# A first load in two parts by partitions, and a reworked tail, in a loss kernel bound by its loads

## Chip, cores, metric

One core of a Trainium2 chip. The metric is the device time of one execution in microseconds; profiles are of single executions, whose span (first to last instruction) is some 2 us shorter.

## The reference

```python
# pred, target: (32, 147, 768) float32
mean = target.mean(axis=-1, keepdims=True)
var = target.var(axis=-1, keepdims=True)
target = (target - mean) / np.sqrt(var + 1e-6)
loss = np.mean((pred - target) ** 2, axis=-1)
return loss.mean(axis=-1)          # 32 numbers
```

Each row of 768 numbers is normalised, subtracted, squared and averaged. Both inputs are read once, 28.90 MB, and 32 numbers are written.

## The kernel before

The 128 partitions are 32 batches x 4 rows; partition 4b + j holds rows 37j and onward of batch b, one row of 768 per "column" c. Columns 0 to 35 fill all partitions, a last one (REST) fills 96. The first four target columns and REST come in float32 from SyncE's queue (the hardware queue); all else goes through GpSimd's queue (the software queue), which converts to bf16 (13.52 MB written there for 27.03 read).

```python
def load(kind, c0, c1, d0, d1, q):
    ...
    til = data.tile([P, (c1 - c0) * w], F32 if q == "hw" else BF16, ...)
    src = bass.AP(tensor=x.tensor, offset=x.offset + c0 * D + d0,
                  ap=[[N * D, B], [KJ * D, J - 1 if c0 == REST else J], [1, (c1 - c0) * w]])
    pin((nc.sync if q == "hw" else nc.gpsimd).dma_start(out=til[:n], in_=src))
...
# statistics on VectorE (two bn_stats and a bn_aggr a column), root on ScalarE,
# normalisation on GpSimd; then, for most columns, TensorE adds -target and +pred
# through identity matrices into PSUM, and ScalarE squares and sums:
    nc.scalar.activation(out=z[:n, :w], in_=z[:n, :w], func=ACTF.Square, accum_out=dest[:n])
# columns 31 and 34 are VectorE's: difference in bf16, then
def mean_of_squares(u, dest):
    z = zs[u]
    mv = small.tile([P, 2], F32, name="mvz")
    bn(mv, [z[:, 0:half], z[:, half:D]])
    nc.vector.scalar_tensor_tensor(out=dest, in0=mv[:, 0:1], scalar=mv[:, 0:1], in1=mv[:, 1:2],
                                   op0=ALU.mult, op1=ALU.add)
...
# at the end a few products with masks sum over partitions, a copy, a store of 128 bytes
```

A small list scheduler in the program orders each engine's instructions by estimated times. The last column (35) is loaded and squared in pieces of 512 and 256.

## Time and profile before

| | before |
|---|---|
| median time | 77.87 us (77.81 to 78.01) |
| span of the profile | 75.9 us |
| first DMA packet | 2.24 us |
| last load's last increment | 72.19 us |
| VectorE, GpSimd, TensorE, ScalarE busy | 66%, 69%, 50%, 42% |
| read from memory | 28.90 MB |

How to read it: no compute engine is near full, the DMA row is. So only what happens before the DMA engines run, how fast they run, and what follows the last landing can move the time. The semaphore of a load of 32 batches rises sixteen times in the trace (the hardware queue's two loads and the store give 16 + 16 + 1 = 33 semaphore writes); this text takes an increment as the share of one of the core's 16 DMA engines, and how far the sixteen lie apart as a sign of how even the engines are. No trace names the engine of a packet or of an increment, so "twelve engines" below means twelve increments. The lines themselves stand in the prediction.

### The profile page before, as it was taken

The numbers are of one execution on the slowest core, as the hardware profiler recorded it, in microseconds if no ns is written. First come the engines' busy times: TensorE is split into PE (matmuls) and PEld (weight loads), VectorE is DVE, ScalarE is ACT, GpSimd is POOL, SyncE is SP. The second block draws the span as 40 slices with busy tenths as digits, with TensorE's granted clock in tenths as the row PEclk, the third lists the DMA queues.
The fourth block names the chain that finished last, engine by engine and source line by source line (L and its number), as shares of the span: only waits on it lengthen the run. The fifth ranks groups of instructions, "written<-read, shape, count | busy, mean of one in ns | idle before, by whom it ended". The sixth has DMA issues, their size and how long they took to land.

```text
span 75.9 us, 638 instructions
## 1 busy us (share of the span) xinstructions
PE 38.2 (50%) x128; PEld 11.5 (15%) x128; DVE 50.2 (66%) x137; ACT 32.0 (42%) x67; POOL 52.6 (69%) x78
## 2 busy tenths in 40 slices
PE   0000000046884865507682877197517978774860
PEld 0000000011222221102110212031102213212230
DVE  0000399999999999997079609941999891019770
ACT  5100000400259519502940096019522963995850
POOL 4998205299999489899399508960999998992000
PEclk9999999999999999999555558955985558999999
DMA  0899999999999999999999999999999999999500
GB/s 0 207 414 330 243 230 236 220 210 207 214 214 223 214 221 210 207 214 217 217 220 217 211 207 217 227 210 196 212 214 214 209 212 213 203 211 200 86 0 0
DMA packets 4118, 15.43 MB, mean 203 GB/s; under 512 B 466, under 2 KB 1458, under 8 KB 3986
## 3 DMA queue, kind: packets, MB, share of 16 engines
q0 software_dynamic: 3856, 13.52, 88.8%
q1 hardware_dynamic: 258, 1.87, 6.9%
q14 instruction: 3, 0.02, 0.1%
q8 instruction: 1, 0.02, 0.1%
HBM read 28.90 MB, written 0.00 MB: 381 GB/s over the span
## 4 chain that ended last, share of the span: by engine, by line
DMA 62%; DVE 13%; POOL 13%; issue 3%; PE 2%; ACT 2%; POOLq 0%; DVEq 0%; ACTq 0%
DMA p<-in_pred_dram 52%; DMA t<-in_target_dram 11%; POOL s L212 10%; DVE st L162 10%; POOL p L108 2%; PE z L226 2%; ACT z L238 2%; DVE mv L163 2%; DVE zd L245 1%; POOL t L108 1%; PE acc L294 0%; DVE r L192 0%; DVE rl L251 0%; DVE mvz L163 0%; ACT r L186 0%
## 5 line engine op out<-in xcount | busy, mean ns | idle before, releaser
L212 POOL TENSOR_SCALAR s<-t,nm,r 128x768 bf16<-128x768 bf16 (+2 forms) x37 | 36.0, 979 | 9.7 <-DVE r L192 7.5
L162 DVE BATCH_NORM_STATS2 st<-t 128x6 f32<-128x384 bf16 (+2 forms) x74 | 36.2, 530 | 9.3 <-DMA t<-in_target_dram 9.3
L238 ACT ACTIVATE z<-z 128x1536 f32<-128x1536 f32 (+4 forms) x21 | 25.7, 1223 | 22.9 <-PE z L226 22.9
L226 PE MATMUL z<-s,nident 128*128 128x512 bf16 (+3 forms) x55 | 19.5, 460 | 25.5 <-POOL s L212 17.8
L226 PE MATMUL z<-p,ident 128*128 128x512 bf16 (+3 forms) x55 | 19.0, 476 | 9.8 <-DMA p<-in_pred_dram 9.7
L108 POOL DMA_DIRECT2D p<-in_pred_dram x18 | 10.3, 575 | 1.0 <-DVE r L192 0.3
L186 ACT ACTIVATE r<-mv,eps_t 128x4 f32<-128x4 f32 (+2 forms) x12 | 3.5, 289 | 17.7 <-DVE mv L163 17.0
L226 PEld LDWEIGHTS <-nident 128*128 128x128 bf16 (+1 forms) x55 | 4.6, 107 | 39.5 <-ACT z L238 18.1
L226 PEld LDWEIGHTS <-ident 128*128 128x128 bf16 (+1 forms) x55 | 6.4, 117 | 20.3 <-issue 17.7
L108 POOL DMA_DIRECT2D t<-in_target_dram x9 | 5.4, 605 | 4.8 <-DMA t<-in_target_dram 3.8
L163 DVE BATCH_NORM_AGGREGATE mv<-st 128x2 f32<-128x12 f32 (+1 forms) x37 | 7.7, 209 | 1.3
L192 DVE RECIPROCAL r<-r 128x4 f32<-128x4 f32 (+2 forms) x12 | 1.7, 143 | 9.3 <-ACT r L186 9.2
L238 ACT ACTIVATION_READ_ACCUMULATOR z<-z 128x1 f32 (+1 forms) x21 | 4.0, 189 | 0.0
L245 DVE TENSOR_TENSOR zd<-p,s 128x768 bf16<-128x768 bf16 x2 | 1.9, 944 | 2.5 <-POOL s L212 2.1
L151 DVE TENSOR_SCALAR mask_mean<-mask 128x32 f32<-128x32 f32 x1 | 2.7, 2731 | 0.0
L187 ACT ACTIVATE nm<-mv 128x4 f32<-128x4 f32 (+2 forms) x12 | 2.3, 191 | 0.0
L162 DVE BATCH_NORM_STATS2 st<-zd 128x6 f32<-128x384 bf16 x4 | 2.0, 552 | 0.1
L186 ACT ACT_TABLE_LOAD x1 | 1.3, 1283 | 0.8 <-PEq L340 0.8
L294 PE MATMUL acc<-mask,rl 128*1 128x32 f32 x10 | 1.1, 192 | 0.2 <-ACT z L238 0.2
L148 DVE MEMSET eps_t<- 128x1 f32 x1 | 0.1, 59 | 0.9 <-PEq L340 0.9
L294 PEld LDWEIGHTS acc<-mask,rl 128*1 128x1 f32 x10 | 0.5, 82 | 0.5 <-ACT z L238 0.3
L294 PE MATMUL acc<-mask_mean,rl 128*1 128x32 f32 x4 | 0.4, 190 | 0.1
(23 smaller groups left out, 4.7 us busy)
## 6 DMA issues: line engine op xcount, KB each, us to landing
t<-in_target_dram POOLq DMA_DIRECT2D x7, 768.0 KB, 26.3
p<-in_pred_dram POOLq DMA_DIRECT2D x5, 768.0 KB, 29.1
p<-in_pred_dram POOLq DMA_DIRECT2D x5, 384.0 KB, 20.0
t<-in_target_dram SPq DMA_DIRECT2D x1, 1536.0 KB, 8.0
p<-in_pred_dram POOLq DMA_DIRECT2D x5, 192.0 KB, 12.3
t<-in_target_dram POOLq DMA_DIRECT2D x2, 384.0 KB, 24.6
t<-in_target_dram SPq DMA_DIRECT2D x1, 288.0 KB, 10.4
p<-in_pred_dram POOLq DMA_DIRECT2D x1, 144.0 KB, 10.6
```

Of the source, the lines that this page charges most:

```text
L108: pin((nc.sync if q == "hw" else nc.gpsimd).dma_start(out=til[:n], in_=src))
L151: op("mask_mean", "DVE", 0.2, ["masks"], lambda: pin(nc.vector.tensor_scalar(out=mask_mean, in0=mask, scalar1=float(D), scalar2=None, op0= ...
L162: pin(nc.vector.bn_stats(out=st[:n, j, :], in_=x))
L163: pin(nc.vector.bn_aggr(out=out, in_=st[:n, :len(parts)]))
L186: pin(nc.scalar.activation(out=r[:n], in_=mv[:n, :, 1], func=ACTF.Sqrt, bias=eps_t[:n], scale=1.0))
L187: pin(nc.scalar.activation(out=nm[:n], in_=mv[:n, :, 0], func=ACTF.Copy, scale=-1.0))
L192: pin(nc.vector.reciprocal(out=rs[g][:n], in_=rs[g][:n]))
L212: pin(nc.gpsimd.tensor_scalar(out=s[:n, so:so + D], in0=til[:n, o:o + D], scalar1=nm, scalar2=r, op0=ALU.add, op1=ALU.mult))
L226: pin(nc.tensor.matmul(z[:n, a:b], eye[:n, :n], src[:n, so + a:so + b], start=first, stop=not first))
L238: pin(nc.scalar.activation(out=z[:n, :w], in_=z[:n, :w], func=ACTF.Square, accum_out=dest[:n]))
L245: pin(nc.vector.tensor_tensor(out=z, in0=til[:, o:o + D], in1=s[:, so:so + D], op=ALU.subtract))
L294: pin(nc.tensor.matmul(acc, vec[:n], m[:n], start=len(turn) == 1, stop=len(turn) == len(finals)))
```

## The change

Its intent: the first load in two parts (its first packets sooner), a shorter chain on VectorE for its tail columns, the last column in equal halves with a PSUM tile of its own, and roots placed ahead of squares that still wait. The core of it:

```diff
+        if not tbuf:
+            h = B // 4
+            for a, b in ((0, h), (h, B)):
+                part = bass.AP(tensor=x.tensor, offset=src.offset + a * N * D,
+                               ap=[[N * D, b - a], [KJ * D, J], [1, (c1 - c0) * w]])
+                pin(eng.dma_start(out=til[a * J:b * J], in_=part))
+        else:
+            pin(eng.dma_start(out=til[:n], in_=src))
...
-    piece("p", KM - 1, KM, 0, BANK)
-    piece("p", KM - 1, KM, BANK, D)
+    piece("p", KM - 1, KM, 0, half)
+    piece("p", KM - 1, KM, half, D)
...
-        mv = small.tile([P, 2], F32, name="mvz")
-        bn(mv, [z[:, 0:half], z[:, half:D]])
-        (multiply and add of mean and variance into dest)
+        pin(nc.vector.scalar_tensor_tensor(out=z, in0=z, scalar=1.0, in1=z, op0=ALU.mult, op1=ALU.mult,
+                                           accum_out=dest))
...
-            key = (t, rank, i)
+            key = (t - (1.0 if name[0] == "root" else 0.0), rank, i)
```

Cut: the scheduler's landing estimates (some 0.7 us later), the last piece's own PSUM tile, and the removal of a mask scaled by 768.

More of the change, by code (lines that the diff above doesn't have):

```diff
@@ L87 @@
     units += [((KM - 6 + i,), 0, D, eng) for i, eng in enumerate(("ACT", "DVE", "ACT", "ACT", "DVE"))]
-    units += [((KM - 1,), 0, BANK, "ACT"), ((KM - 1,), BANK, D, "ACT")]
+    units += [((KM - 1,), 0, half, "ACT"), ((KM - 1,), half, D, "ACT")]
     ops, by_name = [], {}
@@ L107, in load @@
                       ap=[[N * D, B], [KJ * D, J - 1 if c0 == REST else J], [1, (c1 - c0) * w]])
-        pin((nc.sync if q == "hw" else nc.gpsimd).dma_start(out=til[:n], in_=src))
+        eng = nc.sync if q == "hw" else nc.gpsimd
+        if not tbuf:
[6 more added lines that the diff above has]
+            pin(eng.dma_start(out=til[:n], in_=src))
         for c in range(c0, c1):
             KIND[kind].setdefault(c, []).append((d0, d1, til, (c - c0) * w))
-    land, lanes, clock, last = {}, {"hw": [], "sw": []}, 2.5, {}
+    land, lanes, clock, last = {}, {"hw": [], "sw": []}, 2.9, {}
     for i, (kind, c0, c1, d0, d1, q) in enumerate(stream):
         w = (c1 - c0) * (d1 - d0)
-        clock += w * rows_of(c0) / P * 0.915 / D + 0.03
-        lanes[q].append(clock + 0.8)
+        clock += w * rows_of(c0) / P * 0.915 / D + (0.0 if w >= 4 * D else 0.04)
+        lanes[q].append(clock + 1.1)
         for c in range(c0, c1):
-            land[kind, c, d0] = clock + 0.8
+            land[kind, c, d0] = clock + 1.1
         k = len(lanes[q])
@@ L130 @@
     mask_rest = singles.tile([P, B], F32)
-    mask_mean = singles.tile([P, B], F32)
     eps_t = singles.tile([P, 1], F32)
@@ L150 @@
     op("masks", "POOL", 3.0, [], masks, early=3.0)
-    op("mask_mean", "DVE", 0.2, ["masks"], lambda: pin(nc.vector.tensor_scalar(
-        out=mask_mean, in0=mask, scalar1=float(D), scalar2=None, op0=ALU.mult)), rank=99.0)
     mvs = {}
@@ L228, in sub_target @@
     def sub_target(u, d0, w):
-        zs[u, d0] = psum.tile([P, 3 * BANK], F32, name="z")
+        if (u, d0) == units[-1][:2]:
+            zs[u, d0] = psum1.tile([P, BANK], F32, name="z_last")
+        else:
+            zs[u, d0] = psum.tile([P, 3 * BANK], F32, name="z")
         s, so = sbuf[u[0]]
@@ L245, in difference, with square_dve @@
         pin(nc.vector.tensor_tensor(out=z, in0=til[:, o:o + D], in1=s[:, so:so + D], op=ALU.subtract))
-    def mean_of_squares(u, dest):
+    def square_dve(u, dest):
         z = zs[u]
-        mv = small.tile([P, 2], F32, name="mvz")
-        bn(mv, [z[:, 0:half], z[:, half:D]])
-        pin(nc.vector.scalar_tensor_tensor(out=dest, in0=mv[:, 0:1], scalar=mv[:, 0:1], in1=mv[:, 1:2],
-                                           op0=ALU.mult, op1=ALU.add))
+        pin(nc.vector.scalar_tensor_tensor(out=z, in0=z, scalar=1.0, in1=z, op0=ALU.mult, op1=ALU.mult,
+                                           accum_out=dest))
     n_early = sum(1 for u, d0, d1, eng in units if len(u) == 2)
@@ L271 @@
             dest = singles.tile([P, 1], F32, name=f"rl{k}")
-            finals.append((("sq", k), dest, mask_rest if u[0] == REST else mask if eng == "ACT" else mask_mean,
+            finals.append((("sq", k), dest, mask_rest if u[0] == REST else mask,
                            rows_of(u[0])))
@@ L275 @@
             op(("diff", k), "DVE", 0.6, norms, lambda u=u: difference(u), rank=-2.0, early=arrive)
-            op(("sq", k), "DVE", 1.5, [("diff", k)], lambda u=u, dest=dest: mean_of_squares(u, dest), rank=-70.0)
+            op(("sq", k), "DVE", 1.0, [("diff", k)], lambda u=u, dest=dest: square_dve(u, dest), rank=-70.0)
             continue
-        op(("subt", k), "PE", 0.37 * w / D, norms + users[-2:-1] + ["ident"],
+        op(("subt", k), "PE", 0.37 * w / D, norms + (users[-2:-1] if k < len(units) - 1 else []) + ["ident"],
            lambda u=u, d0=d0, w=w: sub_target(u, d0, w), rank=k + 0.0)
@@ L296 @@
     for i, (need, vec, m, n) in enumerate(finals):
-        op(("final", i), "PE", 0.2, [need, "masks", "mask_mean"], lambda v=vec, m=m, n=n: final(v, m, n), rank=90.0)
+        op(("final", i), "PE", 0.2, [need, "masks"], lambda v=vec, m=m, n=n: final(v, m, n), rank=90.0)
     HOP = 0.15
@@ L310 @@
             t = max([free[engine], early] + [end[x] + (0.0 if ops[by_name[x]][1] == engine else HOP) for x in needs])
-            key = (t, rank, i)
+            key = (t - (1.0 if name[0] == "root" else 0.0), rank, i)
             if best is None or key < best[0]:
-                best = (key, i)
-        (t, _, _), i = best
+                best = (key, i, t)
+        _, i, t = best
         name, engine, dur, needs, fn, rank, early = ops[i]
```

## The prediction

> **What bounds the kernel now.** I read the page first, then the chain that ended last in order of time, then the timeline of both ends, then the single DMA packets in the trace. The page:
>
> ```profile
> DVE  0000399999999999997079609941999891019770
> POOL 4998205299999489899399508960999998992000
> DMA  0899999999999999999999999999999999999500
> ...
> q0 software_dynamic: 3856, 13.52, 88.8%
> q1 hardware_dynamic: 258, 1.87, 6.9%
> ...
> HBM read 28.90 MB, written 0.00 MB: 381 GB/s over the span
> ...
> DMA 62%; DVE 13%; POOL 13%; issue 3%; PE 2%; ACT 2%; POOLq 0%; DVEq 0%; ACTq 0%
> ```
>
> The DMA row stands at 9 from the third of its forty slices to the thirty-seventh, while VectorE (66% of the span) and GpSimd (69%) have holes. So the kernel is the time before the DMA engines run, the time they need for 28.90 MB, and what comes after the last landing. The packets give the rate: a 12,288-byte packet takes 0.460 to 0.475 us on its engine, from 3.4 us on and in both queues (a software packet writes 6,144 bytes because it converts to bf16, but reads 12,288). Eight such packets per engine are one load of four columns, and those loads land 3.66 us apart (16.23, 19.87, 23.53 us and so on): 0.458 us a packet. Each engine thus runs back to back at 12,288/0.46 = 26.7 GB/s, sixteen of them at 427 GB/s. No engine has room to take over another's work.
>
> The end, in the timeline:
>
> ```profile
> 71.29 0.56 DVE L245 TENSOR_TENSOR zd<-p,s 128x768 bf16<-128x768 bf16 x1 [0.37 <-DMA p<-in_pred_dram]
> ...
> 71.88 1.02 DVE L162 BATCH_NORM_STATS2 st<-zd 128x6 f32<-128x384 bf16 x2
> 71.90 0.38 PE L226 MATMUL z<-p,ident 128*128 128x512 bf16 x1
> ...
> 72.37 0.58 ACT L238 ACTIVATE z<-z 128x512 f32<-128x512 f32 x1 [0.22 <-PE z L226]
> ...
> 72.54 0.27 PE L226 MATMUL z<-p,ident 128*128 128x256 bf16 x1
> ...
> 72.96 0.38 ACT L238 ACTIVATE z<-z 128x256 f32<-128x256 f32 x1
> ...
> 73.18 0.22 DVE L251 SCALAR_TENSOR_TENSOR rl<-mvz 128x1 f32<-128x1 f32 x1
> 73.26 0.19 ACT L238 ACTIVATION_READ_ACCUMULATOR z<-z 128x1 f32 x1
> 73.45 0.09 PEld L294 LDWEIGHTS acc<-mask_mean,rl 128*1 128x1 f32 x2 [0.26 <-DVE rl L251]
> ...
> 73.51 0.22 PE L294 MATMUL acc<-mask,rl 128*1 128x32 f32 x2
> 73.77 0.18 DVE L322 COPY ob<-acc 1x32 f32<-1x32 f32 x1 [0.37 <-PE acc L294]
> ```
>
> (I left out lines between.) Column 34 lands at 71.19 us and goes through VectorE until 73.40; the two pieces of column 35 land at 71.86 and 72.19 and go through TensorE and ScalarE until 73.45. **Two chains end within 0.05 us of each other**, so shortening one alone gives nothing. From the last landing to the end of the span it is 75.9 - 72.19 = 3.7 us, of which 2.4 are the last product, the output's copy and its store.
>
> The sixteen increments of the last load's semaphore arrive between 71.08 and 71.73 us, but for one at 72.19: an engine that carried a 16,384-byte instruction fetch at 67.77 us for 0.95 us. It is late from then on.
>
> The start, in the timeline:
>
> ```profile
> 0.81 1.31 SPq L108 DMA_DIRECT2D t<-in_target_dram  x2
> ...
> 8.86 1.02 DVE L162 BATCH_NORM_STATS2 st<-t 128x6 f32<-128x384 f32 x2 [7.92 <-DMA t<-in_target_dram]
> ```
>
> The first packet moves at 2.24 us; packets of the software queue join at 5.74 us, and from there the two queues alternate. The first load has landed at 8.84.
>
> [...] the 258 hardware packets are 128 + 96 of data, one store and 33 semaphore writes, 16 + 16 + 1. [...] the subtraction of column 31, begun at 67.96 beside GpSimd, took 1.33 us, that of column 34 with GpSimd idle 0.56.
>
> **The change part by part.**
>
> First load in two. The parts' patterns begin with 8 and 24 batches. [...] Before, every engine had 128/16 = 8. [...] All later loads are spread evenly and every engine is full to the end, [...] 4 x 0.46 = **1.84 us on every later landing**, the last one included. What may be won back: the first packets of before took about 1 us instead of 0.46 with all sixteen starting at once, and a shorter first issue or fewer starters may save up to 0.4; I put 0.2. And if the engine with the instruction fetch isn't among the eight, the last landing is 71.73 + 1.84 at most instead of 72.19 + 1.84, that is 0.46 less; at even odds 0.23. Shift of the last landing: 1.84 - 0.2 - 0.23 = +1.4 us.
>
> The first load itself: 101 of its 128 packets had begun by 5.74, 6.3 per engine. After, 5.7 of 12 would be left, alternating with software packets at 0.94 a pair: 5.4 us, so it lands at about 11.3 instead of 8.84. VectorE starts 2.5 us late. It has some 26 us idle in the span, and loses the mask multiplication (2.7 us in the table of groups, once), so this is hidden.
>
> VectorE's tail columns. Removed per column: two statistics (1.02), an aggregation (0.22), a small multiply (0.23), with gaps 1.53 us. Added: one multiply over 768 elements with accumulation. Estimate: the statistics run 384 elements in 0.53 and the one-element multiply takes 0.22, [...] plus 0.1 to 0.2 for reading the accumulator: 1.15. Saves about 0.4 us on the chain of column 34, which then ends near 73.0 on before's clock, off the path.
>
> Last column in halves. ScalarE took 0.58 for 512 and 0.38 for 256 columns; 384 is 0.48. With L the last landing, the first half lands near L - 0.5 and its square runs from L - 0.03 to L + 0.45; the second half's product (0.33 and some 0.1 of delay) is ready at L + 0.47, its own PSUM tile sparing it a wait; square and accumulator read end at L + 1.2, against 73.45 - 72.19 = 1.26 before. Gain 0.05 to 0.2; I take 0.15.
>
> Roots ahead of waiting squares, and later estimated landings: these change orders only. Products and squares in the middle have slack against the DMA engines, so 0.
>
> Sum: 77.87 + 1.4 - 0.15 = **79.1 us**.
>
> **Rivals.**
> First, the load is spread over all sixteen engines after all. For it: the new estimates of landing in the program (2.9 and 1.1 us) agree with before's measured landings within some 0.1 us, as if the split had moved nothing. [...] Then the tail alone counts: 77.5 to 77.8.
> Second, the engines share a bound, so that the others go faster [...]. [...] Against it: the constant 0.46 us a packet. It would make about 78.
> Third, GpSimd stalls on issues: it waits in order for the eighth-last load to land, and the program now expects landings 1.8 us too early. Its last normalisation ended at 68.88, 2.3 us before column 34 landed, so I see little; if it bites, 79.5 to 80.
> Fourth, the tail's gain is larger (roots unblock ScalarE, 0.3 us more). It can't reach the 1.56 us that a gain of 2% needs.
>
> **Range and chances.** I give the uneven spread 80%. Within it the time runs from 78.7 (start and fetch both kind) to 79.7, and 2% slower is 79.43, so about a third of it is beyond. The rest lies at 77.4 to 78.2. Range 77.5 to 79.7; slower 0.27, same 0.69, faster 0.04.
>
> **What would show it.** Semaphore writes of the hardware queue: 8 + 12 + 16 + 1 = 37 if the spread is uneven, 49 if all parts use sixteen engines. Increments of the later loads then spread over some 4 us or more instead of 0.5, and loads land about 1.6 us later from 16 us to the end. The first statistics begin near 11 us. In the tail there is one multiply of about 1 us and an accumulator read in place of four instructions, VectorE is done before ScalarE, and the last square ends 1.2 us after the last landing. The prediction is wrong if the landings in the middle stand where they stood, or if the tail after the last landing changes by over 0.4 us.

Its sum came to 77.87 + 1.4 - 0.15 = 79.1 us. The four extra packets behind the 1.84 in that 1.4 have lost their derivation: the prediction took 12 packets of the first load for eight engines, 8 for four and none for four from an assumption that no trace had shown by then. The result shows the counts: the two parts' semaphores rise 8 and 12 times, and later loads have twelve late increments and four on time. The middle step of the multiply's estimate (1.0 us) assumed a fixed time per instruction that is not measured; that multiply is not in the sum.

## The result

84.1 us median (83.7 to 84.88, 6 runs) against 77.86 before: ratio 1.0813, 95% interval 1.0765 to 1.0861. A ratio here is the mean time of one kernel's fast runs over that of the other's fast runs of the same rounds, so not quite the ratio of the medians. The change is 6.2 us slower; 1.2 were predicted.

The page of the changed kernel (VectorE's and the DMA engines' busy tenths, the queues, the chain that ended last):

```profile
DVE  0000000009999999995995970893399974015520
DMA  0699999999999999999999999999999999998300
...
q1 hardware_dynamic: 262, 1.87, 10.4%
...
HBM read 28.90 MB, written 0.00 MB: 347 GB/s over the span
...
DMA 65%; DVE 14%; POOL 8%; PE 3%; ACT 3%; issue 2%; SPq 1%; ACTq 0%; POOLq 0%; DVEq 0%
```

The DMA row is as full as before and the bytes are the same, yet the hardware queue's 1.87 MB take 10.4% of the engines' time instead of 6.9%: **the same packets last longer**. VectorE starts five slices (some 10 us) later. The hardware packets number 262, four more than before: 8 + 12 + 16 + 1 = 37 semaphore writes instead of 33 (the first part's semaphore rises 8 times from 5.26 to 5.86 us, the second's 12 times from 17.59 to 18.48).

The start, in its timeline:

```profile
0.82 1.73 SPq L115 DMA_DIRECT2D t<-in_target_dram  x2
...
17.32 0.56 POOL L117 DMA_DIRECT2D t<-in_target_dram  x1 [9.15 <-DMA t<-in_target_dram]
18.58 1.02 DVE L167 BATCH_NORM_STATS2 st<-t 128x6 f32<-128x384 f32 x2 [17.64 <-DMA t<-in_target_dram]
```

The first statistics begin at 18.58 us, not at 8.86, and GpSimd stood 9.15 us before an issue that needed an earlier load landed. The stages, as windows of time (busy time per engine, then the granted clock, the DMA engines' busy share and GB/s written), before and after:

```profile
2.00:4.00 2.00, 0.00 (x0) 0.00 (x0) 0.00 (x0) 0.09 (x1) 2.00 (x5) 1.00 0.93 258
4.00:6.00 2.00, 0.00 (x0) 0.00 (x0) 0.00 (x0) 0.00 (x0) 2.00 (x5) 1.00 0.99 402
...
12.00:16.00 4.00, 0.11 (x1) 0.10 (x1) 3.86 (x14) 0.78 (x4) 2.23 (x4) 1.00 1.03 213
```

```profile
2.00:4.00 2.00, 0.00 (x0) 0.00 (x0) 0.00 (x0) 0.09 (x1) 2.00 (x5) 1.00 0.62 123
4.00:6.00 2.00, 0.00 (x0) 0.00 (x0) 0.00 (x0) 0.00 (x0) 2.00 (x5) 1.00 1.01 221
...
12.00:16.00 4.00, 0.00 (x0) 0.00 (x0) 0.00 (x0) 0.00 (x0) 0.00 (x0) 1.00 1.07 173
```

Busy shares are alike from 4 us on. GB/s counts bytes written, and a software packet writes half of what it reads, so the row from 4 to 6 us says little: before it is almost all hardware packets, after it is a mixture. The row from 12 to 16 us does tell: before all its packets are software's, at 213 GB/s written; after, with hardware packets among them, it is 173. A busy DMA engine is not always one that moves bytes at its pace.

The loss is complete by 22 us. The load of target columns 8 to 11 increments its semaphore between 15.71 and 16.23 us before; after, four engines do at 15.42 to 16.28 and twelve at 22.00 to 22.88. From there to the last loads those twelve stay 6.2 to 6.7 us behind (the increments of a load in order of time, compared one by one), and the other four within 0.3 us of before until the last few loads.

The 128 packets of 12,288 bytes of the first load, read one by one in the trace:

| start | before | after |
|---|---|---|
| 2 to 6 us | 105 packets, 0.46 to 0.48 from 4 us on | 32 (the first part), 0.46 to 0.49 from 4 us on |
| 6 to 8 us | 23, 0.473 | 20, mostly 0.473 |
| 8 to 16 us | none | 76, 0.70 to 1.38, mean 1.095 |

The second part's first packets moved at 6.3 us, after the first part's last increment at 5.86. The sum, per engine: 76 packets on twelve engines are 6.3 each, 6.3 x (1.095 - 0.467) = **4.0 us**; REST's packets, 72 of them at 0.223 instead of 0.134, give 6 x 0.089 = **0.5 us**; on the eight engines of the first part the four extra packets give 4 x 0.46 = **1.84 us**. Together 6.3 us, against 6.2 in the times. The first two terms are what the prediction did not have. This sum is an average and explains less than it seems to: it takes the 76 packets as even over twelve engines, and its last term belongs to eight engines alone, while all twelve are 6.2 to 6.7 us late. How the other four lost as much is not resolved. It also leaves out the software packets, which last 1,102.9 us in sum instead of 1,079.3.

### The profile page after: what moved, and what is told of

The parts are those of the page before. It is cut to its first block, busy times and chain, and to the rows that moved or that the text cites. A ratio compares the mean times of both kernels' runs of the same rounds, so it can differ in the third digit from the quotient of the medians.

```text
span 83.2 us, 636 instructions
## 1 busy us (share of the span) xinstructions
PE 36.9 (44%) x128; PEld 11.4 (14%) x128; DVE 45.9 (55%) x132; ACT 32.7 (39%) x67; POOL 52.5 (63%) x78
## 3 DMA queue, kind: packets, MB, share of 16 engines
q1 hardware_dynamic: 262, 1.87, 10.4%
HBM read 28.90 MB, written 0.00 MB: 347 GB/s over the span
## 4 chain that ended last, share of the span: by engine, by line
DMA 65%; DVE 14%; POOL 8%; PE 3%; ACT 3%; issue 2%; SPq 1%; ACTq 0%; POOLq 0%; DVEq 0%
DMA t<-in_target_dram 50%; DMA p<-in_pred_dram 16%; DVE st L167 11%; POOL s L217 7%; DVE mv L168 3%; PE z L231 2%; ACT z L246 2%; POOL p L117 1%; SPq L115 1%; ACT z_last L246 1%; PE acc L300 1%; ACT r L191 0%; DVE r L197 0%; DVE ob L329 0%; ACTq L361 0%
## 5 line engine op out<-in xcount | busy, mean ns | idle before, releaser
L231 PE MATMUL z<-s,nident 128*128 128x512 bf16 (+4 forms) x54 | 18.9, 454 | 36.3 <-POOL s L217 26.9
L246 ACT ACTIVATE z<-z 128x1536 f32<-128x1536 f32 (+3 forms) x20 | 25.2, 1258 | 6.7 <-PE z L231 6.4
L231 PE MATMUL z<-p,ident 128*128 128x512 bf16 (+4 forms) x54 | 17.9, 460 | 7.1 <-DMA p<-in_pred_dram 7.1
L253 DVE TENSOR_TENSOR zd<-p,s 128x768 bf16<-128x768 bf16 x2 | 1.1, 559 | 6.2 <-POOL s L217 4.5
L257 DVE SCALAR_TENSOR_TENSOR zd<-zd 128x768 bf16<-128x768 bf16 x2 | 1.9, 958 | 0.1
```

The source lines that it names most:

```text
L231: pin(nc.tensor.matmul(z[:n, a:b], eye[:n, :n], src[:n, so + a:so + b], start=first, stop=not first))
L246: pin(nc.scalar.activation(out=z[:n, :w], in_=z[:n, :w], func=ACTF.Square, accum_out=dest[:n]))
L253: pin(nc.vector.tensor_tensor(out=z, in0=til[:, o:o + D], in1=s[:, so:so + D], op=ALU.subtract))
L257: pin(nc.vector.scalar_tensor_tensor(out=z, in0=z, scalar=1.0, in1=z, op0=ALU.mult, op1=ALU.mult, accum_out=dest))
```

## The experiments

**Theory:** the loss is unevenness (1.84 us, as predicted) plus a slowdown of packets that depends on which partitions are written at the same time. By the theory, 81 to 82 us for `extra_other` and up to 85 for `four8`; without it, 6 us lost in `sw_split`. A, B, C and D below are partitions 0 to 31, 32 to 63, 64 to 95 and 96 to 127, and the runs tell on which of them a part has longer packets. The whole load, on A to D at once, had 0.46 to 0.48 us from 4 us on (the kernel before). **Rivals:** the rest of the change; loads on fewer than sixteen engines being slow as such; the reads.

### Is it the split?

`nosplit`: the changed kernel with its first load whole.

```diff
-        if not tbuf:
-            (two parts)
+        pin((nc.sync if q == "hw" else nc.gpsimd).dma_start(out=til[:n], in_=src))
```

> The changed kernel with the first load in one piece again. Both theories of the loss [...] say that the split costs all of it: 77.5 to 77.8 us, loads landing as in the kernel before (last one near 72.2 us), hardware packets back to 0.46 us. The rival, that the new order of roots and issues or the multiply with accumulation costs something, says well over 78.2 us.

77.76 us, ratio 0.9969 (0.9925 to 1.0013). `splitonly`, the kernel before with the split alone:

> The kernel before with the split of the first load alone. If the split is the whole loss: 83.7 to 84.9 us, and twelve engines' shares of every later load some 6.2 us late. If the rest of the change has a part in it: clearly under 83 us.

84.34 us, ratio 1.082 (1.075 to 1.0891), and again twelve engines 6.2 to 6.6 us late. **The split is the whole loss**; the rest of the change is worth at most a few tenths.

### Splits over all partitions

`cols` splits by columns, each part on all partitions:

```diff
-            for a, b in ((0, h), (h, B)): (parts of batches)
+            cw = (c1 - c0) * w // 2
+            for a in (0, cw): (all batches, out=til[:, a:a + cw])
```

> The changed kernel with the first load split into two by columns, every part on all 128 partitions. [...] both theories say 77.5 to 78 us and packets of 6144 bytes at about 0.25 us; the rival that any second hardware load in front costs time, or that two parts for one tile hurt, says over 79 us.

77.64 us, ratio 0.9964 (0.9908 to 1.0021). `rows4` splits by partitions, but part j takes every fourth one, `out=til[j::J]`, so that each part reaches over A to D.

> The changed kernel with the first load in four parts by partitions, part j taking every fourth partition, so 32 batches and sixteen engines in each [...]. [...] 77.5 to 78.2 us, packets of 0.46. If splitting by partitions is itself what costs (as the two halves did, 79.8): 79 us or more.

77.86 us, ratio 0.9945 (0.9881 to 1.0008). From 3 us on most packets take 0.46 to 0.47 us. Neither several parts nor parts of 32 partitions cost anything as such, in these two runs.

### Half the partitions at a time, without unevenness

`half16`: `h = B // 2`, so 16 batches and sixteen engines a part (274 hardware packets, 49 of them semaphore writes, 16 + 16 + 16 + 1); A and B first, then C and D.

> The changed kernel with the first load split into two equal halves of 16 batches, so sixteen engines each and 8 packets an engine as before. Uneven engines alone: 77.5 to 78 us, hardware packets of 0.46 us. [...] hardware packets near 0.93 us, so 8 x 0.46 = 3.7 us more on every engine, 81 to 82.5 us, all sixteen increments of a load staying close together.

79.83 us, ratio 1.0248 (1.0186 to 1.031). The slowdown came, the size was too large. Of the packets that started between 4 and 5.5 us, before the software queue joined, all 26 took **0.94 to 0.97 us**, twice 0.47; in the second part, with software packets between, 0.75. All sixteen increments of later loads stay together, 2.0 us late, and its 12,288-byte packets last 100.5 us in sum against 67.7 of `nosplit`: 32.8/16 = 2.05 us an engine. Its windows from 2 to 6 us:

```profile
2.00:4.00 2.00, 0.00 (x0) 0.00 (x0) 0.00 (x0) 0.09 (x1) 2.00 (x5) 1.00 0.99 227
4.00:6.00 2.00, 0.00 (x0) 0.00 (x0) 0.00 (x0) 0.00 (x0) 2.00 (x5) 1.00 0.90 184
```

Engines 90% busy at 184 GB/s, against 99% and 402 before, with hardware packets alone up to 5.6 us in both: for their busy time half the bytes (184/0.90 = 204 GB/s against 402/0.99 = 406).

`mid16` moves that part by 8 batches: first batches 8 to 23 (partitions 32 to 95, that is B and C), then 0 to 7, then 24 to 31.

```diff
-            for a, b in ((0, h), (h, B)):
+            for a, b in ((h, 3 * h), (0, h), (3 * h, B)):
```

> The changed kernel with the first load in parts of batches 8 to 23, 0 to 7 and 24 to 31, in this order. The first part has sixteen engines[...]. [...] packets of 0.46 us from the second round on. If partitions 32 to 63 share a path with 64 to 95 in this case [...]: 0.92 us for the first part's packets. The time itself[...] 79.5 us or more.

One look, state unknown: 80.59 us. The first part's packets from 3.5 us on take 0.46 to 0.57. The same number of batches, engines and bytes as in a half, other partitions, half the duration: **which partitions are written decides**. Its cost, eight increments some 2.8 us late, is the unevenness of the other two parts (its 49 semaphore writes are 16 + 8 + 8 + 16 + 1; with both eights on the same engines, as the eight late increments suggest, 12 packets there and 4 on the others: 1.9 us) and longer packets in the last part (median 0.79 us, 0.9 us more on each of eight engines).

### Reads, or bytes written?

The software queue reads the same 12,288 bytes a packet and writes 6,144. The first load went there, whole (`sw_whole`), in halves (`sw_half16`) and in 8 and 24 batches (`sw_split`).

```diff
-    piece("t", 0, 4, q="hw")
+    piece("t", 0, 4)
```

> The changed kernel with its first load whole and in the software queue, which converts to bf16, so that every packet still reads 12288 bytes and writes 6144. Only the base for the next two runs: near 78 us, packets of 0.474 us, all engines even.

> The same, with the first load in two halves of 16 batches: sixteen engines each[...], the same reads, half the bytes written. [...] packets stay near 0.474 and the time within 0.4 us of the whole load. If the slow packets came from the reads or from the engines' assignment: packets of 0.7 us and more and 2 us lost, as with the hardware queue.

> The same, with the change's split into 8 and 24 batches. Unevenness alone[...]: at most 12 packets of the load on an engine instead of 8, so 1.9 us more than the whole load, with packets of 0.474. [...]

Whole 77.45 us (ratio 0.9943, 0.9908 to 0.9977), halves 77.53 (0.9945, 0.9918 to 0.9972), 8 and 24 79.76 (1.0235, 1.0201 to 1.0269). The halves cost nothing, with packets of 0.474; the window of `sw_half16`:

```profile
4.00:6.00 2.00, 0.00 (x0) 0.00 (x0) 0.00 (x0) 0.00 (x0) 1.80 (x4) 1.00 1.05 212
```

212 GB/s written, so twice that read, where the hardware halves managed 184 in all. **Half the bytes written, and the loss of the halves is gone.** That speaks for the write side, though the queue changed along with the bytes. The split into 8 and 24 is not as clean: it lost 2.3 us against 1.9 expected, and its trace shows more than unevenness. Of its 6,144-byte packets that started between 6 and 11 us, 40 of 145 took over 0.55 us, up to 1.86 (in `sw_whole` none of 167), and in later loads twelve increments, not eight, come 2.2 to 2.9 us later than in `sw_whole`. What makes these packets long is not shown.

### Unevenness alone

`extra_own` and `extra_other`: the first load whole, and ahead of it its first 8 batches once more into a spare tile, on partitions 0 to 31 or 64 to 95.

```diff
+            spare = data.tile([P, (c1 - c0) * w], F32, name="spare")
+            (source: the first 8 batches)
+            pin(nc.sync.dma_start(out=spare[p0:p0 + B], in_=part))    # p0 = 0 or 64
```

> The changed kernel with the first load whole, and ahead of it a load of its first 8 batches once more into a spare tile on partitions 0 to 31, never used[...]. It measures unevenness alone: 4 x 0.46 = 1.84 us on half of each load's increments, 79.3 to 79.8 us, hardware packets staying at 0.46. If a load on fewer than sixteen engines is slow in itself: packets near 1 us and over 81 us.

> The same spare load, same source, same engines, but into partitions 64 to 95[...]. Unevenness alone: as in the run before it, 79.3 to 79.8 us. [...] A slow read side would make both runs equal, for they read the same rows.

79.73 us (ratio 1.0211, 1.0159 to 1.0263) and 79.91 (1.0244, 1.0195 to 1.0292). In `extra_own` eight increments of most later loads come 1.7 to 2.0 us later than in `nosplit`, most packets at 0.47: that is the predicted term for 4 packets. But the other eight come 2.2 to 2.9 us later. The likely reason is that the engines without a spare packet had nothing to move before 3.45 us (2.24 in the kernel before), and that software packets which started between 4.4 and 4.8 us took 1.03 to 1.18 us. So the 1.9 us of the whole run are not a measure of the four packets alone.

In `extra_other` the spare packets met no other hardware packets, since the whole load's first one moved only at 6.38 us, when they were through. They did meet software packets, and there the trace shows a difference after all. Of the spare packets that started from 4.2 us on, all twelve took 0.51 to 0.67 us; in `extra_own` all eleven took 0.46 to 0.49. The two runs read the same rows, and only the partitions written differ: **the slowdown is on the write side**.

### Other splits

`four8` puts the first load on eight engines, in four parts of 8 batches (274 hardware packets again, the 49 semaphore writes now 4 x 8 + 16 + 1):

```diff
+            for a, b in ((0, h), (h, 2 * h), (2 * h, 3 * h), (3 * h, B)):
```

> The changed kernel with the first load in four parts of 8 batches[...]. Unevenness alone: 8 x 0.46 = 3.7 us late on eight engines, 81.2 to 81.7 us, packets of 0.46. [...] If fewer engines are slow in themselves: packets near 1 us from the first, over 86 us.

84.12 us (ratio 1.0803, 1.0729 to 1.0877). The unevenness, with 16 packets on those engines instead of 8, is 8 x 0.46 = 3.7 us; the packets of the first part are 0.46 to 0.50 after the first ones, of the second 0.46 to 0.74, of the last two (C, then D) mostly 0.65 to 0.89 (medians 0.79 and 0.80); what makes these longer is not shown. In sum the 128 packets last 86.3 us instead of 67.7 in `nosplit`, 2.3 us more on each of eight engines; 3.7 and 2.3 make 6.0, against 6.3 seen. Eight engines are not slow as such: the first part shows it.

`parts12` (parts of 12, 12 and 8 batches) has, by the author's count, the change's 12, 8 and 0 packets an engine, and its first part writes A with half of B; in `parts9` (9, 9, 9, 5) the first part writes A with 4 partitions of B; `order24` runs the change's 24 batches (B, C and D) first.

```diff
+            for a, b in ((0, 12), (12, 24), (24, B)):                     # parts12
+            for a, b in ((0, 9), (9, 18), (18, 27), (27, B)):             # parts9
+            for a, b in ((h, B), (0, h)):                                 # order24
```

> The changed kernel with the first load in parts of 12, 12 and 8 batches[...]. [...] less than the change loses, 80.5 to 83 us. [...] If all packets of a load move in step: all 48 near 0.9. Engine count as the cause: as slow as the change, 84 us.

> The changed kernel with the first load in parts of 9, 9, 9 and 5 batches. [...] If the packets of one load move in step, all 36 of its packets from the third round on take 0.9 us[...]. [...] Either way slow, [...] unevenness alone is 3.7 us, 81.5 us and more.

> The changed kernel with its two parts the other way round, the part of 24 batches first. It then runs from 2.4 us[...]. [...] If a load of eight packets an engine moves in step: hardly any at 0.46. The time should be near the change's 84 us, or up to 2 us less.

82.64 us (ratio 1.0602), then 84.72 and 84.17 in one look each, state unknown. `parts12` loses 1.5 us less than the change, by that count with the same unevenness. Of its first 48 packets 22 took over 0.9 us after the first twelve (a load's first packets are slow in all these runs, 0.79 to 1.56 us in the change). In `parts9` only 2 of the first part's packets from 3.7 us on took 0.9, the rest 0.46 to 0.56: **packets of a load do not move in step**, and the less of B is written beside A, the fewer are slow (all 26 looked at in `half16`, 22 in `parts12`, 2 here). But in `order24` the part of 24 batches shows, from 4 to 7.5 us, 1.05 to 1.43 us for all but one of its 29 packets. 12 x 12,288 bytes in 1.37 us are 108 GB/s, about four times the 26.7 of one engine. B and C together had packets of 0.46 to 0.57 (`mid16`), so the third of this part that is on B might have been spared; C and D together are the second part of `half16` (0.75). **Why hardly any packet is spared stays open**, and so does why they take more than the 0.94 to 0.97 us of `half16`. It is in the change too, where all twelve end within 0.9 us. So what the halves show of the partitions explains the change's part of 24 batches only in part. In its later loads `order24` does keep two losses apart: four increments are 4.8 to 4.9 us later than in `nosplit` and eight are 6.8 to 7.2, and those 2 us more are about what four extra packets should cost.

### A faster version

`sw_fewer`: `sw_whole` with five two-column loads of pred joined to two of four columns and one of two.

> A version meant to beat both kernels: the changed kernel with the first load whole and in the software queue, and the last ten two-column pieces of the prediction input but one pair joined into loads of four columns (packets of 0.474 us for four columns against 0.248 for two, so 8 columns x 8 packets save about 0.35 us of every engine). Expected 77.0 to 77.4 us against 77.45 without the joining.

78.54 us, ratio 1.0073 (1.003 to 1.0115): slower than before. The last landing did not move (72.12 against 72.16 us in `sw_whole`), so the saving of packets did not come; why was not looked for. The coarser loads put ScalarE behind: its last square starts at 74.05 us instead of 72.63 (timelines of `sw_whole`, then `sw_fewer`).

```profile
72.63 0.48 ACT L237 ACTIVATE z_last<-z_last 128x384 f32<-128x384 f32 x1
```

```profile
74.05 0.48 ACT L236 ACTIVATE z_last<-z_last 128x384 f32<-128x384 f32 x1
```

**`sw_whole` beats both kernels**: 0.6% faster than before, with its interval clear of 1.

## Why the prediction was wrong

**What bounds the kernel: right.** 28.90 MB through sixteen engines that did not take over from each other: from 22 us on twelve stayed 6.2 to 6.7 us late and, until the last few loads, four within 0.3 us of before. The loss stayed to the end.

**First load in two: the spread was right, the price was not.** Engines: 8 and 12, as the 37 semaphore writes show. Four extra packets: 1.84 us predicted; eight increments were 1.7 to 2.0 us late in `extra_own`. **The step that failed is the sum "1.84 - 0.2 - 0.23 = +1.4 us"**, which has no term for packets that last longer. It took the constant 0.46 us as the engine's own property and drew from it that an engine's rate doesn't depend on the others. That held where each part lay on A to D (`rows4`: 0.46 to 0.47 us; `cols`: no time lost). Measured in its place: 1.095 us a packet for 6.3 packets, 4.0 us, and 0.5 us for REST's. The longer packets are measured; that the partitions written bring them is shown for the halves and `extra_other`, and open in part for the change's own 24 batches. What was to be won back, 0.2 us at the start and 0.23 by the fetch, did not come: first packets took 0.79 to 1.56 us, and the late engine of the fetch is among the late twelve (78.70 us, the next 78.24).

**First load's landing: wrong for the same reason.** First statistics at 18.58, 11.3 predicted. That this is hidden behind VectorE's slack fits the trace: 55% busy, and the last landings lag those of before by no more than the ones at 22 us do.

**VectorE's tail: right, a little better.** The timeline of `nosplit`, which has the change's tail without its split:

```profile
71.48 0.56 DVE L244 TENSOR_TENSOR zd<-p,s 128x768 bf16<-128x768 bf16 x1 [1.86 <-DMA p<-in_pred_dram]
...
72.07 0.96 DVE L248 SCALAR_TENSOR_TENSOR zd<-zd 128x768 bf16<-128x768 bf16 x1
...
72.37 0.47 ACT L237 ACTIVATE z<-z 128x384 f32<-128x384 f32 x1
72.42 0.32 PE L222 MATMUL z_last<-p,ident 128*128 128x384 bf16 x1
...
72.85 0.48 ACT L237 ACTIVATE z_last<-z_last 128x384 f32<-128x384 f32 x1
72.96 0.08 DVE L248 DVE_READ_ACCUMULATOR zd<-zd 128x1 f32 x1
...
73.26 0.19 ACT L237 ACTIVATION_READ_ACCUMULATOR z_last<-z_last 128x1 f32 x1
```

0.96 + 0.08 us; predicted were 1.0 and 0.1 to 0.2. VectorE ends at 73.04, 0.41 before ScalarE: its chain is off the path, as said.

**Last column in halves: right in `nosplit`, missed in the change's own profile.** In `nosplit` the last landing is at 72.38, and the last accumulator read ended at 73.45: 1.07 us, 1.2 predicted, 1.26 before. From the last landing to the end of the span 3.5 us instead of 3.7: a gain of 0.2, 0.15 predicted. The profile of the changed kernel itself shows a window and two lines that say otherwise:

```profile
78.00:80.00 2.00, 2.00 (x12) 0.58 (x11) 1.31 (x3) 1.27 (x3) 0.00 (x0) 0.50 0.02 2
...
79.33 0.53 PE L231 MATMUL z_last<-p,ident 128*128 128x384 bf16 x1
...
80.52 0.19 ACT L246 ACTIVATION_READ_ACCUMULATOR z_last<-z_last 128x1 f32 x1
```

Its last landing is at 78.70, so the read ended 2.0 us after it, and the span 4.5 us after it: 0.7 more than before, which the prediction named as a sign of being wrong. The granted TensorE clock was 0.50 from 78 to 80 us and the last product took 0.53 us, not 0.32 (in `nosplit` the clock was 1.00 from 72 to 74 us). This execution is the slowest of the six, 84.88 us against a median of 84.1. The clock is the likely reason; no run tests it.

**Roots and orders: as predicted, nothing to be seen** in the sum; no run takes them alone.

**Rivals.** Even spread: refuted. A shared bound that lets others go faster: refuted, the packets took longer (1.095 us) and the four engines on time gained nothing (within 0.3 us of before until the last few loads). GpSimd's stalls: they came (9.15 us at once), and no cost of them is seen: the twelve late engines fall no further behind after 22 us. The range's top, 79.7, was the worst case of unevenness; a rival "packets get longer" was not among the four, and the 0.27 for slower was far too low for it.

## What to carry to other kernels

When a load is cut by partitions, look in the trace how many increments each part has, how long its packets take and which partitions it writes together: here an equal cut into halves cost 2.0 us and one into 8 and 24 batches 6.2, while cuts by columns or by every fourth partition cost nothing. Where all DMA engines are full to the end, what some of them carry extra at the start can stay to the end: here twelve engines' 6.2 to 6.7 us. A busy DMA engine proves no progress (1.07 busy at 173 GB/s after, 1.03 at 213 before): read the duration of single packets beside it, and bytes per time only between stretches whose packets write the same share of what they read.

## What stays open

With sixteen engines on a hardware load the software queue's first packet came at 5.74 us; after the change, with eight on the first part, it came at 3.03, and with two packets an engine in the first part (`rows4`) at 3.51. What sets these times is open, and so is when a second load of one hardware queue begins: after the change the second part's first packet moved at 6.30 us, after the first part's last increment at 5.86, yet REST's packets began at 7.8 us while the second part's ran to 17.1.
